# FoX heads first, differential heads last: reordering a mixer's attention stage

## The chip, the cores and the metric

The kernel runs on one core of a Trainium2 chip. A core has TensorE (PE, matrix products; its weight loads are listed as PEld), VectorE (DVE), ScalarE (ACT), GpSimd (POOL), SyncE (SP, which here only issues DMAs) and DMA queues. The metric is the device time of one execution in microseconds, the median of several runs; lower is better.

## The reference

Two layers, each of three residual blocks, then one RMSNorm, on x of 512 tokens by 1024 columns in float32:

```
x = x + 1/2 * SwiGLU_1(RMSNorm(x))
x = x + W_out [FoX_heads(h) ; Diff_heads(h)],   h = RMSNorm(x)
x = x + 1/2 * SwiGLU_2(RMSNorm(x))
```

The mixer, the middle block, has two groups of causal heads that read the same h through one input projection:

```
FoX, 8 heads of 64:  s = q k^T / 8 + cum[query] - cum[key];  o_f = softmax(s) v
                     cum = cumulative sum of log_sigmoid(h w_ff + bias)
Diff, 4 heads:       two maps of 64 on rope(q), rope(k);  v has 128 columns
                     o_d = (softmax(s1) - lam * softmax(s2)) v
                     o_d = RMSNorm(o_d) * subln * (1 - lambda_init)
out = [o_f ; o_d] W_out
```

So a FoX head needs the forget sums `cum`, a diff head needs rope, two softmaxes and, at its end, a norm over its 128 columns. Rows 0 to 511 of W_out belong to FoX, rows 512 to 1023 to diff.

## The kernel before

**Precision.** Every float32 product is made as three matmuls of a high and a low part (`mm3`, lines 399 to 403): high by high, high by low, low by high. Weights arrive in 128 x 1024 blocks of 512 KB and are split on ACT (high part, a cast, L83) and DVE (low part, a subtraction, L84). The feed-forward blocks use a seven-product scheme and are not touched by the change.

**Order of work.** The kernel is Python that emits instructions for each engine; a list scheduler of the compiler then fixes the order of each engine's queue, with the emitted order as priority and what is ready (in its own timing) ahead of what is not. A tile name has one buffer or a few; a new use waits until the old one is over. PSUM has 8 banks: 3 under the tag "a", 5 under "b".

**Weights.** `stream` lists all weight blocks in the order of use; `next_w(ahead)` hands out the next one and splits up to `ahead` further ones. In the mixer three buffers (G0 to G2) hold split blocks, three (R0 to R2) raw ones. The blocks of the input projection come from `w_in` in a fixed order, the first four of W_out go into the tiles XA0 to XA3, which until then hold h.

**The mixer.** `mixer` runs one projection (`proj`, `head`) and then a loop over 12 units, one per head, with 4 steps each (one for each block of 128 queries). A step s does, for unit s // 4, the scores and softmax of one query block (`softmax_step`); five steps later the transposes of the probabilities (`trans_step`); a step after that, a part of P·V (`pv_step`). Between these, `fill_to` draws on one long generator, `filler`, which holds all TensorE work that is not attention: projections, V of both kinds, gates, and the output projection as far as it can be had early. Filler is counted in matmuls: a projection is 48, V of one kind 96, the gates 16. `LEAD` is the filler issued ahead of the loop, `TARGET[u]` what must have been issued when unit u + 1 begins; what is left after the loop runs in `run(fill)`, then `out_rest` finishes the output projection and makes the next feed-forward's input forms.

**Before the change** units 0 to 3 are diff heads, 4 to 11 FoX heads. The filler is: projection d1, V of diff, d2, gates, d3 and f0 (with the gates' two later parts in between), V of FoX, f1 to f3, and 84 matmuls of output projection (`out_early`), 628 in all.

**Steps at the end of a head.** A FoX pair: ACT copies half of P·V, DVE adds, `split_o` splits the sum (L909 ACT, L910 DVE) into the operand `ovt[k]` of the output projection. A diff head: copy (L934), square (L936), split of the squares (L938, L939), then, a step later, `stats`: two matmuls with ones (L944, L945) and ACT (L946). After the last diff head `diff_norm` runs: the mean squares go to DRAM (L969) and back in another layout (L972), square root and reciprocal, to DRAM (L976), back as a broadcast to 128 partitions per head (L980), a multiplication (L982) and `split_o`. These are four DMA hops in a row.

**Evictions.** A projection's PSUM is scaled by DVE (FoX, L804), or put through rope (diff, L797, L798), where a DMA of four pieces turns the partitions (L801) and DVE adds (L802). Then q is split (L775, L776); k is first duplicated by DMA (L786), then split (L787, L788).

**Output projection.** `GROUPS` are the four 128 x 512 results of tokens 0 to 255, `GR2` those of tokens 256 to 511; each sums over k = 0 to 7, of which 0 to 3 are FoX and 4 to 7 diff. Before, early output takes k = 4, 5, 6, 7, 0, 1, 2 of the first half; `out_rest` adds k = 3, then makes the second half with k = 4 to 7, 3, 1, 0, 2.

Of the kernel before, what the change touches and what calls it, by code (L numbers as in the profile page):

```python
# [8 lines left out]
F32 = mybir.dt.float32  # L9
# [6 lines left out]
P = 128  # L16
# [13 lines left out]

LEAD = 70
TARGET = [128, 238, 290, 344, 393, 490, 497, 522, 525, 552, 560, 590, 604, 616]

# [19 lines left out]
def trunk(ctx, tc, xT, x, gains, gain_row, w_gu, w_dn, w_in, w_ff, w_out, fbias, lams, subln, consts, rope, out):  # L53
# [160 lines left out]
    len_x = list(range(KP)) * DEPTH  # L214
    OUT_K = (4, 5, 6, 7, 0, 1, 2)
    for n in range(2 * DEPTH):
        l = n // 2
        if n % 2 == 1:
            for i in range(24 + len(OUT_K)):
                k = OUT_K[i - 24] if i >= 24 else None  # L220
                tag = MIX[i % 3] if i < 24 else None if k >= 4 else MIX[(i - 28) % 3]
                stream.append(plain(w_in[l, i] if i < 24 else w_out[l, k], f"R{(i + 1) % 3}", tag))
        r = 0
        for kind, c in PARTS:
            if (n, kind, c) != (0, "u", 0):
                r = (gu_units if kind == "u" else dn_units)(n, c, part_order(kind, c), r)
# [368 lines left out]
    def mixer(l, n_next, mid):  # L595
# [27 lines left out]
        def y_pair(i):  # L623
            return ys[i // 4][:, i % 4], ys[i // 4][:, 4 + i % 4]
        os_ = [home(f"w{i}", [P, 2, S], F32, f"o{i}") for i in range(2)]

# [90 lines left out]
        def gates():  # L717
            pz = psum("a")
            for k in range(KT):
# [33 lines left out]
            yield 0  # L753
            pc = psum("a")
            for t in range(NB):
# [87 lines left out]

        cbs = {}

        def softmax_step(u, qb):
# [66 lines left out]
        def pv_step(u, kb):  # L913
# [97 lines left out]
        def out_early():  # L1011
            for i, k in enumerate(early):
                take_wo(k)
                for g in GROUPS[:3]:
                    if i == 0:
                        po1[g] = psum("a")
                    out_mm(po1[g], g, 0, k, i == 0, False)
                    yield 3
            g = GROUPS[3]
            po1[g] = psum("b")  # L1020
            for i, k in enumerate(early):
                out_mm(po1[g], g, 0, k, i == 0, False)
                yield 3
            take_wo(2)
            for g in GROUPS:
                out_mm(po1[g], g, 0, 2, False, False)
                yield 3

        def out_rest():
            busy.difference_update(LENT)  # L1030
            got = home("R2", [P, 1024], F32, "raw")
            sp.dma_start(out=got, in_=w_out[l, 3])
            w3 = home("G3", [P, 2, 1024], F32R, "wg")
            wo[3] = split(got, w3[:, 0], w3[:, 1])
            ensure(1)
            for g in GROUPS:
                out_mm(po1[g], g, 0, 3, False, True)
                out_add(po1[g], g, 0)
            GR2 = [(t, c) for c in range(2) for t in range(2)]
            po2 = {g: psum("a" if i < 3 else "b") for i, g in enumerate(GR2)}  # L1040
# [6 lines left out]
            for k in (3, 1):  # L1047
                for g in GR2:
                    out_mm(po2[g], g, 1, k, False, False)
            for g in GR2:  # L1050
                for k in (0, 2):
                    out_mm(po2[g], g, 1, k, False, k == 2)
                out_add(po2[g], g, 1)
            live.difference_update(MIX)
# [5 lines left out]

        early = [4, 5, 6, 7, 0, 1]

        def filler():
            yield from proj(("d", 1))
            yield from diff_v()
            yield from proj(("d", 2))
# [5 lines left out]
            for p_, n in ((proj(("d", 3)), 3), (proj(("f", 0)), 3)):  # L1072
# [4 lines left out]
            yield from fox_v()  # L1077
            for j in range(1, 4):
                yield from proj(("f", j))
# [366 lines left out]
```

## Time and profile before

| | us |
|---|---|
| median of 3 runs | 1865.27 (1864.65 to 1866.11) |
| the profiled execution | 1866.57 |
| its span, first to last instruction | 1864.8 |
| TensorE busy in the span | 1832.3 |
| DVE busy | 1611.7 |
| ACT busy | 1137.3 |

The first layer's mixer runs from about 346 to 600 us, its loop of heads from 374 to 569; the second layer's from about 1269 to 1524. Engine names are as above; "PE idle before" a line is time in which TensorE waited, with the instruction that released it. Matmuls overlap in the pipeline, so a single one is listed with some 0.39 us although one starts every 0.225 us, and a busy TensorE is not always one at its full rate. A window row gives busy time and, after x, the number of instructions that touch the window.

### The profile page before, as it was taken

What the parts mean: (1) busy time and instruction counts of PE and PEld (TensorE: products, weight loads), DVE (VectorE), ACT (ScalarE), POOL (GpSimd) and SP (SyncE); (2) the same over time, 40 slices, a digit from 0 to 9 for tenths busy, and PEclk for the clock granted to TensorE, in tenths of its full rate; (3) what the DMA queues carried; (4) which work ended last, traced back from release to release, by engine and by line L of the source; (5) the groups of instructions that cost most, each with busy time, mean ns of one, the idle gap of its engine ahead of it and who ended that gap; (6) DMA issues with size and microseconds to landing.
All of it is one profiled execution on the core that took longest, in us unless ns stands there. A gap on an engine that the chain in (4) does not pass through costs nothing.

```text
span 1864.8 us, 24528 instructions
## 1 busy us (share of the span) xinstructions
PE 1832.3 (98%) x8702; PEld 1495.9 (80%) x8702; DVE 1611.7 (86%) x2531; ACT 1137.3 (61%) x1819; POOL 128.1 (7%) x154
## 2 busy tenths in 40 slices
PE   9999999999999999999999999999999999999997
PEld 5888888778868889888878988887777688888886
DVE  7898899878686999898998989997877869898998
ACT  7555555557795755566575556545576957455564
POOL 2010000000000100100000000000000000000101
PEclk9999999999999999999999999999999999999999
DMA  9786655343336775777567667533433467756742
GB/s 314 207 225 192 186 141 145 99 127 103 108 97 180 204 203 152 193 213 193 136 179 205 170 163 213 157 115 112 120 97 109 128 170 193 214 142 186 222 115 89
DMA packets 95530, 303.80 MB, mean 163 GB/s; under 512 B 12568, under 2 KB 15128, under 8 KB 95408
## 3 DMA queue, kind: packets, MB, share of 16 engines
q1 hardware_dynamic: 74816, 232.15, 36.9%
q0 software_dynamic: 19296, 68.17, 20.6%
q10 hardware_dynamic: 1296, 1.93, 0.3%
q8 instruction: 68, 1.11, 0.2%
q14 instruction: 54, 0.44, 0.1%
HBM read 287.45 MB, written 2.16 MB: 155 GB/s over the span
## 4 chain that ended last, share of the span: by engine, by line
PE 82%; DVE 10%; ACT 6%; DMA 1%; issue 1%; SPq 0%; DVEq 0%; ACTq 0%
PE ps_c L401 12%; PE ps_c L402 12%; PE ps_c L403 12%; PE ps L401 8%; PE ps L402 8%; PE ps L403 8%; PE ps_a L401 3%; PE ps_a L402 3%; PE ps_a L403 3%; DVE wg L84 3%; PE ps_t L497 2%; DVE x L526 1%; PE ps_g L1265 1%; ACT wg L83 1%; ACT pg L876 1%
## 5 line engine op out<-in xcount | busy, mean ns | idle before, releaser
L83 ACT CAST wg<-raw 128x1024 fp32r<-128x1024 f32 (+1 forms) x525 | 537.8, 1032 | 480.0 <-PE ps L403 172.5
L84 DVE TENSOR_TENSOR wg<-raw,wg 128x1024 fp32r<-128x1024 f32 (+1 forms) x525 | 619.6, 1190 | 105.3 <-ACT wg L83 102.2
L401 PE MATMUL ps_c<-wg,xf 128*128 128x512 f32 (+1 forms) x736 | 277.9, 378 | 2.0 <-ACT wg L83 1.6
L402 PE MATMUL ps_c<-wg,xf 128*128 128x512 f32 (+1 forms) x736 | 277.1, 377 | 0.5 <-DVE wg L84 0.5
L403 PE MATMUL ps_c<-wg,xf 128*128 128x512 f32 (+1 forms) x736 | 276.4, 376 | 0.0
L401 PE MATMUL ps<-wg,xf 128*128 128x512 f32 (+1 forms) x552 | 210.1, 381 | 0.0
L402 PE MATMUL ps<-wg,xf 128*128 128x512 f32 (+1 forms) x552 | 207.3, 376 | 0.9 <-DVE wg L84 0.9
L403 PE MATMUL ps<-wg,xf 128*128 128x512 f32 (+1 forms) x552 | 206.7, 376 | 0.0
L401 PEld LDWEIGHTS ps_c<-wg,xf 128*128 128x128 f32 x736 | 138.7, 189 | 28.8 <-ACT wg L83 2.0
L402 PEld LDWEIGHTS ps_c<-wg,xf 128*128 128x128 f32 x736 | 139.0, 189 | 26.1 <-DVE wg L84 1.0
L403 PEld LDWEIGHTS ps_c<-wg,xf 128*128 128x128 f32 x736 | 138.9, 189 | 25.1
L134 POOL DMA_DIRECT2D raw<-w_gu x86 | 74.6, 867 | 1130.7 <-DMA raw<-w_gu 597.6
L401 PE MATMUL ps_c<-wg,hf 128*128 128x512 f32 x352 | 138.4, 393 | 4.0 <-DVE x L526 4.0
L402 PE MATMUL ps_c<-wg,hf 128*128 128x512 f32 x352 | 137.4, 390 | 0.0
L403 PE MATMUL ps_c<-wg,hf 128*128 128x512 f32 x352 | 137.1, 390 | 0.0
L526 DVE SCALAR_TENSOR_TENSOR x<-ps_c,x 128x512 f32<-128x512 f32 x192 | 124.0, 679 | 1.3 <-PE ps_c L403 1.2
L402 PEld LDWEIGHTS ps<-wg,xf 128*128 128x128 f32 x552 | 104.0, 188 | 18.9 <-DVE wg L84 1.3
L403 PEld LDWEIGHTS ps<-wg,xf 128*128 128x128 f32 x552 | 103.8, 188 | 18.9
L401 PEld LDWEIGHTS ps<-wg,xf 128*128 128x128 f32 x552 | 103.9, 188 | 18.0 <-ACT xf L83 0.4
L401 PE MATMUL ps_a<-XA,wg 128*128 128x512 f32 x256 | 106.0, 415 | 1.9 <-ACT XA L355 1.8
L401 PE MATMUL ps<-wg,hf 128*128 128x512 f32 x264 | 103.0, 390 | 0.0
L402 PE MATMUL ps<-wg,hf 128*128 128x512 f32 x264 | 103.0, 390 | 0.0
(290 smaller groups left out, 3549.6 us busy)
## 6 DMA issues: line engine op xcount, KB each, us to landing
raw<-w_gu SPq DMA_DIRECT2D x218, 512.0 KB, 4.6
raw<-w_dn SPq DMA_DIRECT2D x100, 512.0 KB, 4.2
raw<-w_gu POOLq DMA_DIRECT2D x86, 512.0 KB, 7.0
raw<-w_in SPq DMA_DIRECT2D x48, 512.0 KB, 3.3
raw<-w_dn POOLq DMA_DIRECT2D x40, 512.0 KB, 5.6
kdup<-qk_t SPq DMA_DIRECT2D x64, 128.0 KB, 2.4
raw<-w_out SPq DMA_DIRECT2D x16, 512.0 KB, 3.2
raw<-w_dn SPq DMA_DIRECT2D x20, 256.0 KB, 5.6
```

Of the source, the lines that this page charges most:

```text
L83: act.copy(out=hi, in_=src)
L84: dve.tensor_tensor(out=lo, in0=src, in1=rf(hi), op=ALU.subtract)
L134: pool.dma_start(out=t, in_=where(two, h)[1], accum_op=ALU.add)
L401: pe.matmul(p, lh, rh, start=start, stop=False, skip_group_check=again)
L402: pe.matmul(p, lh, rl, start=False, stop=False, skip_group_check=again)
L403: pe.matmul(p, ll, rh, start=False, stop=stop, skip_group_check=again)
L497: pe.transpose(pj[j][:, e * 256 + p * P:e * 256 + (p + 1) * P], hs[j][p][:, o:o + P], ident)
L526: dve.scalar_tensor_tensor(out=xc, in0=src, scalar=scale, in1=xc, op0=ALU.mult, op1=ALU.add)
L876: act.activation(out=e, in_=e, func=AF.Exp, scale=-1.0, bias=st[:, 0:1], accum_out=st[:, 2:3])
L1265: pe.matmul(pg[2 * half + j], gained(kp, e, half)[:, j * P:(j + 1) * P], w0[kp][:, e * S:(e + 1) * S], start=kp + e == 0, stop=kp == KP - ...
```

## The change

The units change places: FoX heads are units 0 to 7, diff heads 8 to 11. All that hangs on the order follows.

- The first projection is f0. The filler is: gates, V of FoX (with the gates' later parts inside), f1 to f3, d0, d1, V of diff, d2, d3, early output; 580 matmuls. `LEAD` is 92, `TARGET` new.
- Blocks of `w_in` and W_out are stored and streamed in that order; the k that go to XA0 to XA3 are 0 to 3.
- Early output is 36 matmuls, k = 0 to 3 for three groups; the splits of k = 4, 5, 6 follow. `out_rest` loads k = 7, then makes the fourth group with k = 0 to 3, the second half with k = 0, 1, the first half with k = 4 to 7, the second half with k = 2 to 7. All second-half sums and the fourth group lie in PSUM banks "b".
- The forget sums, which were broadcast into the rope tables' buffer, have their own (w1), and FoX outputs theirs (w0); the diff outputs take w0 and w1 over when those are done. V of diff lies in the other half of the y tiles. The gates use banks "b".

The number of matmuls, splits, evictions and bytes is the same.

```diff
-LEAD = 70
-TARGET = [128, 238, 290, 344, 393, 490, 497, 522, 525, 552, 560, 590, 604, 616]
+LEAD = 92
+TARGET = [137, 186, 213, 241, 267, 296, 321, 350, 410, 520, 560, 574, 580]
...
-    OUT_K = (4, 5, 6, 7, 0, 1, 2)
+    OUT_K = tuple(range(KT - 1))
...
-                tag = MIX[i % 3] if i < 24 else None if k >= 4 else MIX[(i - 28) % 3]
+                tag = MIX[i % 3] if i < 24 else None if k < 4 else MIX[(i - 28) % 3]
...
-        os_ = [home(f"w{i}", [P, 2, S], F32, f"o{i}") for i in range(2)]
+        os_ = {}
...
-                vh, vl = y_pair(t)
+                vh, vl = y_pair(4 + t)
...
-                wh, wl = next_w(2 if name != ("f", 3) else 1 - c)
+                wh, wl = next_w(2 if name != ("d", 3) else 1 - c)
...
-        units = [("d", h) for h in range(DIFF_H)] + [("f", h) for h in range(FOX_H)]
+        units = [("f", h) for h in range(FOX_H)] + [("d", h) for h in range(DIFF_H)]
...
+        cb_t = home("w1", [P, 2, S], F32, "cb")
+        fo_t = home("w0", [P, 2, S], F32, "fo")
...
-                    cbs[h] = rope_t[h % 2]
+                    cbs[h] = cb_t[:, h % 2]
...
+                if h % 2 == 0:
+                    os_[h // 2] = home(f"w{h // 2}", [P, 2, S], F32, f"o{h // 2}")
...
-                if h % 2 == 0:
-                    fo["u"] = pm_tile()
+                fo["u"] = fo_t[:, h // 2 % 2]
...
         def out_early():
-            for i, k in enumerate(early):
+            for k in range(4):
                 take_wo(k)
                 for g in GROUPS[:3]:
...
-            take_wo(2)
-            for g in GROUPS:
-                out_mm(po1[g], g, 0, 2, False, False)
-                yield 3
+            for k in (4, 5, 6):
+                take_wo(k)
...
+            g = GROUPS[3]
+            po1[g] = psum("b")
+            for k in range(4):
+                out_mm(po1[g], g, 0, k, k == 0, False)
+            GR2 = [(t, c) for c in range(2) for t in range(2)]
+            po2 = {}
+            for k in (0, 1):
+                for g in GR2:
+                    if k == 0:
+                        po2[g] = psum("b")
+                    out_mm(po2[g], g, 1, k, k == 0, False)
             for g in GROUPS:
-                out_mm(po1[g], g, 0, 3, False, True)
+                for k in (4, 5, 6, 7):
+                    out_mm(po1[g], g, 0, k, False, k == 7)
                 out_add(po1[g], g, 0)
...
-            for k in (4, 5, 6, 7):
+            for k in (2, 3):
                 for g in GR2:
-                    out_mm(po2[g], g, 1, k, k == 4, False)
+                    out_mm(po2[g], g, 1, k, False, False)
...
+            gt = gates()
...
+            fv = fox_v()
+            for n in (3, 18):
                 for _ in range(n):
-                    yield next(p_)
+                    yield next(fv)
                 next(gt)
-                yield from p_
...
+            yield from fv
+            for name in (("f", 1), ("f", 2), ("f", 3), ("d", 0), ("d", 1)):
+                yield from proj(name)
+            yield from diff_v()
+            for name in (("d", 2), ("d", 3)):
+                yield from proj(name)
             yield from out_early()
...
-        head = proj(("d", 0), first=True)
+        head = proj(("f", 0), first=True)
...
-        [qd[:, :4], v_blocks(dv), qd[:, 4:], qf[:, :2], v_blocks(fv), qf[:, 2:]], 1))
+        [qf[:, :2], v_blocks(fv), qf[:, 2:], qd[:, :4], v_blocks(dv), qd[:, 4:]], 1))
```

More of the change, by code (lines that the diff above doesn't have):

```diff
@@ L717, in gates @@
         def gates():
-            pz = psum("a")
+            pz = psum("b")
             for k in range(KT):
@@ L753, in gates @@
             yield 0
-            pc = psum("a")
+            pc = psum("b")
             for t in range(NB):
@@ L1011, in out_early @@
         def out_early():
-            for i, k in enumerate(early):
+            for k in range(4):
                 take_wo(k)
                 for g in GROUPS[:3]:
-                    if i == 0:
+                    if k == 0:
                         po1[g] = psum("a")
-                    out_mm(po1[g], g, 0, k, i == 0, False)
+                    out_mm(po1[g], g, 0, k, k == 0, False)
                     yield 3
[L1019 to L1022, printed above, removed]
-                yield 3
-            take_wo(2)
-            for g in GROUPS:
-                out_mm(po1[g], g, 0, 2, False, False)
-                yield 3
+            for k in (4, 5, 6):
+                take_wo(k)
         def out_rest():
@@ L1031, in out_rest @@
             got = home("R2", [P, 1024], F32, "raw")
-            sp.dma_start(out=got, in_=w_out[l, 3])
-            w3 = home("G3", [P, 2, 1024], F32R, "wg")
-            wo[3] = split(got, w3[:, 0], w3[:, 1])
+            sp.dma_start(out=got, in_=w_out[l, 7])
+            w7 = home("G3", [P, 2, 1024], F32R, "wg")
+            wo[7] = split(got, w7[:, 0], w7[:, 1])
             ensure(1)
+            g = GROUPS[3]
+            po1[g] = psum("b")
+            for k in range(4):
+                out_mm(po1[g], g, 0, k, k == 0, False)
+            GR2 = [(t, c) for c in range(2) for t in range(2)]
+            po2 = {}
+            for k in (0, 1):
+                for g in GR2:
+                    if k == 0:
+                        po2[g] = psum("b")
+                    out_mm(po2[g], g, 1, k, k == 0, False)
             for g in GROUPS:
-                out_mm(po1[g], g, 0, 3, False, True)
+                for k in (4, 5, 6, 7):
+                    out_mm(po1[g], g, 0, k, False, k == 7)
                 out_add(po1[g], g, 0)
-            GR2 = [(t, c) for c in range(2) for t in range(2)]
-            po2 = {g: psum("a" if i < 3 else "b") for i, g in enumerate(GR2)}
-            for k in (4, 5, 6, 7):
+            for k in (2, 3):
                 for g in GR2:
-                    out_mm(po2[g], g, 1, k, k == 4, False)
+                    out_mm(po2[g], g, 1, k, False, False)
             for kp in range(KP):
@@ L1046, in out_rest @@
             squares(0)
-            for k in (3, 1):
+            for k in (4, 5):
                 for g in GR2:
@@ L1050, in out_rest @@
             for g in GR2:
-                for k in (0, 2):
-                    out_mm(po2[g], g, 1, k, False, k == 2)
+                for k in (6, 7):
+                    out_mm(po2[g], g, 1, k, False, k == 7)
                 out_add(po2[g], g, 1)
@@ L1058, in run @@
                 pass
-        early = [4, 5, 6, 7, 0, 1]
         def filler():
-            yield from proj(("d", 1))
-            yield from diff_v()
-            yield from proj(("d", 2))
             gt = gates()
@@ L1071, in filler @@
                 yield w
-            for p_, n in ((proj(("d", 3)), 3), (proj(("f", 0)), 3)):
+            fv = fox_v()
+            for n in (3, 18):
                 for _ in range(n):
-                    yield next(p_)
+                    yield next(fv)
                 next(gt)
-                yield from p_
-            yield from fox_v()
-            for j in range(1, 4):
-                yield from proj(("f", j))
+            yield from fv
[4 more added lines that the diff above has]
+                yield from proj(name)
             yield from out_early()
-        head = proj(("d", 0), first=True)
+        head = proj(("f", 0), first=True)
         for _ in range(KT // 2):
```

## The prediction

> **What bounds the kernel now.** I read the page first (busy shares, chain), then busy time by stretch, TensorE's waits, and the groups of the attention stage.
>
> ```profile
> PE 1832.3 (98%) x8702; PEld 1495.9 (80%) x8702; DVE 1611.7 (86%) x2531; ACT 1137.3 (61%) x1819; POOL 128.1 (7%) x154
> PE 82%; DVE 10%; ACT 6%; DMA 1%; issue 1%; SPq 0%; DVEq 0%; ACTq 0%
> ```
>
> TensorE is busy 98% of 1864.8 us, and the change adds and removes no matmul. It can only move holes. The stretches show where the holes of one mixer are (columns: stretch, its length, then PE, PEld, DVE, ACT, POOL busy, granted clock, DMA share, GB/s):
>
> ```profile
> 629.00:645.00 16.00, 16.00 (x71) 13.03 (x70) 14.38 (x17) 8.13 (x9) 2.60 (x3) 1.00 0.91 252
> 374.00:505.80 131.80, 131.50 (x642) 105.28 (x641) 101.20 (x261) 89.58 (x190) 0.00 (x0) 1.00 0.37 111
> 505.80:569.40 63.60, 59.54 (x321) 45.26 (x320) 52.81 (x138) 54.52 (x132) 0.00 (x0) 1.00 0.41 131
> 530.00:540.00 10.00, 8.40 (x50) 6.32 (x49) 8.82 (x28) 9.79 (x27) 0.00 (x0) 1.00 0.49 138
> 570.00:580.00 10.00, 10.00 (x45) 8.28 (x45) 5.10 (x7) 4.12 (x7) 3.09 (x4) 1.00 0.96 288
> 1430.00:1481.00 51.00, 47.42 (x256) 36.09 (x254) 41.84 (x119) 44.58 (x112) 0.00 (x0) 0.97 0.32 96
> ```
>
> In a pure matmul stretch 71 matmuls take 16 us: 0.225 us for 512 columns, 0.44 ns a column. The attention loop runs from 374 to 569.4. Up to 505.8 (diff heads, then two FoX heads) TensorE is full. From 505.8, where the last six FoX heads run with hardly any filler, ACT is the bound: 9.79 of 10 us at 530. The ends of that stretch are these rows (scores' mask matmul of FoX unit 6, last P·V matmul):
>
> ```profile
> L841 PE MATMUL ps_b<-maskw,identb x24: 219/229/231, 506.0 to 555.9; 128*128 128x128 bf16 x24
> L928 PE MATMUL ps_b<-pt,vf x8: 278/323/387, 508.0 to 569.2; 128*128 128x256 f32 x8
> ```
>
> **Term A, what is removed.** A FoX unit needs on TensorE 2816 columns of scores, 2816 of P·V, 1280 of transposes and 512 of mask: 3.3 us. A diff unit needs 5632, 4224, 1280 and 1024 (sums of squares): 5.3 us. From unit 6 to the end the loop holds six units' scores (7.8 us with masks), seven of transposes and P·V (12.6) and 131 matmuls of filler (628 in all, 497 issued before unit 6; 29.5): 49.9 us in 63.6. The good stretch holds 427 of filler (96.1), four diff units (21.3), two FoX scores (2.6) and some 2 us of odds: 122 in 131.8, an overhead of 8%. At that rate the last six units would take 53.9. So **A = -9.7 us** a mixer if the hole closes.
>
> **Term B, the new tail.** With diff heads last, what ends the mixer is no longer the short FoX eviction. It is, in order: the eviction of the last projection (d3, done at filler 544 of 580, while its unit 11 is due at 560), unit 11's softmax, its P·V, then the diff norm with four DMA hops, which so far ran under FoX projections.
>
> The d eviction goes through two DMA rounds; one K half in the first layer:
>
> ```profile
> 408.62 0.69 DVE L797 TENSOR_TENSOR qk_b<-ps_a,rope 128x512 f32<-128x512 f32 x1 [0.42 <-PE ps_a L403]
> 409.34 2.41 SPq L801 DMA_DIRECT2D qk_c<-qk_b  x4
> 415.24 2.42 SPq L786 DMA_DIRECT2D kdup<-qk_t  x4
> 421.97 0.68 DVE L788 TENSOR_TENSOR qk<-kdup,qk 128x512 fp32r<-128x512 f32 x1
> ```
>
> That is 14.0 us from 408.62 to 422.65 in a crowded stage; without some 2 us behind other DVE work I take 12. The softmax of a diff unit is bound by ACT:
>
> ```profile
> L858 ACT ACTIVATE pg<-pg,st 128x128 f32<-128x128 f32 (+3 forms) x32 | 17.8, 557 | 15.0 <-DVE st L856 14.8
> L858 ACT ACTIVATION_READ_ACCUMULATOR pg<-pg,st 128x1 f32 x32 | 6.0, 189 | 0.0
> L863 ACT ACTIVATE pg<-pg,st 128x128 f32<-128x128 f32 (+3 forms) x16 | 9.0, 562 | 2.8 <-DVE st L862 2.6
> L897 ACT CAST pair<-ps_b 128x512 fp32r<-128x512 f32 (+2 forms) x36 | 16.9, 475 | 6.9 <-PE ps_b L888 6.5
> L936 ACT ACTIVATE osq<-ps_b 128x512 f32<-128x512 f32 x4 | 2.4, 596 | 0.0
> L938 ACT CAST pair<-osq 128x512 fp32r<-128x512 f32 x4 | 2.5, 627 | 0.0
> ```
>
> Per query block two exps and a scaling, 2 x 0.75 + 0.56 = 2.06; four blocks 8.2, and about 2.8 for the first block to pass scores, row minimum and combination: 11. Transposes, casts (0.475 each) and P·V of the last unit: 3.5. Copy, square, cast and subtract of its output: about 2.5. Then the norm, here from its first matmul to the split output of the first head, with the two last hops of the second layer:
>
> ```profile
> 495.98 0.40 PE L944 MATMUL ps_b<-pair,ones 128*32 128x512 f32 x1
> 496.64 0.68 ACT L946 ACTIVATE bb<-ps_b,eps_t 32x512 f32<-32x512 f32 x1 [0.17 <-PE ps_b L945]
> 511.55 1.41 DVE L982 SCALAR_TENSOR_TENSOR ou<-o,sub_s,rbd 128x512 f32<-128x512 f32 x2 [0.30 <-DMA rbd<-ms_d]
> 512.98 0.69 DVE L910 TENSOR_TENSOR y<-ou,y 128x512 fp32r<-128x512 f32 x1
> 1429.59 3.05 DMA ms_d<-nd
> 1432.66 3.31 DMA rbd<-ms_d
> ```
>
> 495.98 to 513.67 is 17.7 us. Sum: 12 + 11 + 3.5 + 2.5 + 17.7 = 46.7 us from d3's last matmul to the first output matmul of a diff head (k = 4).
>
> TensorE's work for that time: 36 matmuls of early output (8.1); 36 that the new order puts ahead of k = 4 (fourth group with k = 0..3, second half with k = 0, 1: 8.1); 24 of k = 2, 3, written behind k = 4 but ready earlier (5.4); three quarters of unit 10's scores and all of unit 11's (4.5); transposes, P·V and sums of units 10 and 11 (5.7), rest of unit 9 (0.7). 32.5, with 8% overhead 35.1. **B = +11.6.** The 24 count only if the compiler's list scheduler, which fixes each queue's order, draws them forward. It does such things: of the 16 transposes that the code writes ahead of the k = 3 products, eight run after them:
>
> ```profile
> 587.06 1.04 PE L339 MATMUL ps_t<-ident,x 128*128 128x128 f32 x8
> 587.86 0.47 PE L401 MATMUL ps_a<-wg,y 128*128 128x512 f32 x1
> 596.60 0.65 PE L339 MATMUL ps_t<-ident,x 128*128 128x128 f32 x4
> ```
>
> Bounds of B: 5 if d3 runs so far ahead of its unit that its 12 us hide under unit 10's softmax; 17 if the 24 stay behind.
>
> **Term C, the FoX units with filler.** Units 2 to 7 get some 28 matmuls each: TensorE 3.3 + 6.3 = 9.6, with overhead 10.4 us. DVE, from
>
> ```profile
> L874 DVE CUSTOM_DVE_ANT_0 pg<-ps_b,rope 128x128 f32<-128x128 f32 (+3 forms) x32 | 15.3, 484 | 3.1 <-PE ps_b L841 2.6 <-PE ps_a L403 0.3
> L898 DVE TENSOR_TENSOR pair<-ps_b,pair 128x512 fp32r<-128x512 f32 (+2 forms) x36 | 19.7, 551 | 8.4 <-ACT pair L897 8.2
> L84 DVE TENSOR_TENSOR wg<-raw,wg 128x1024 fp32r<-128x1024 f32 x21 | 25.7, 1222 | 4.0 <-ACT wg L83 3.9
> L797 DVE TENSOR_TENSOR qk_b<-ps_a,rope 128x512 f32<-128x512 f32 x6 | 4.0, 686 | 0.6 <-PE ps_a L403 0.6
> ```
>
> about 5.9 a unit plus, for a d projection of 48, 2 x 1.22 + 10 passes of 0.68 = 9.3, so 5.4 for 28: 11.3. Neighbouring instructions overlap (DVE's groups of the loop sum to some 174 us, busy is 154), so 10.0: 96% of TensorE's time in units 5 to 7, where FoX softmax meets rope evictions; ACT, the same way, 9.1. DVE will now and then be late: **C = +1** (0 to 4).
>
> **Moved at no cost.** The gates go ahead of the first unit, into the lead (92). Their DVE chain meets no softmax there, and 33 matmuls of V and 48 of projection f1 cover the forget sums' broadcast (4.2 us); without cover its 4.2 would be paid once. The rope DMAs and the gates' DMAs change places on SP's queue among loads that are three blocks ahead. The norm's hops now stand on SP ahead of the load of the last output weights and of the next feed-forward's: if all those wait for the norm, ten loads of 0.5 MB at 288 GB/s take 18 us, under 96 matmuls (21.6 us) that remain after it; POOL's accumulating loads follow these.
>
> ```profile
> raw<-w_gu SPq DMA_DIRECT2D x218, 512.0 KB, 4.6
> rope<-cum_d SPq DMA_DIRECT2D x16, 256.0 KB, 4.2
> ```
>
> **Term D, the clock.** In the second layer the starved stage was granted 0.97 over 51 us: 3 us at half clock, 1.5 us lost; the first layer lost none. A tail with holes in both layers: **D = +0.8** each. No wait of TensorE was long:
>
> ```profile
> PE ps_c L401 <- DVE x L526: 4.0, 4, 1.4
> PE ps_b L927 <- ACT pair L897: 3.9, 6, 0.9
> PE ps_c L401 <- ACT wg L83: 1.6, 1, 1.6
> ```
>
> The Trainium skill (TensorE: Matmul & The Clock Gate, "HAM oscillation — how this bites in real kernels") wants no idle gap beyond about 3.4 us, or the array drops to half clock; the trace shows the drop even with gaps of at most 1.6 us, so here the page is milder than the measurement. By its window, one unbroken gap in each norm would cost half of 3.4 us (an estimate from that page): D 1.7, the sum 1.8 us higher.
>
> **Sum.** -9.7 + 11.6 + 1 + 0.8 = +3.7 a mixer, +7.4 for two layers. The profiled execution took 1866.6 (span 1864.8 plus 1.8 around it), 1.3 above the median of the runs; 1865.3 + 7.4 = **1872.7**. Its own range: B from 9 to 15 gives 1867 to 1880.
>
> **Rivals.** (1) The tail is covered. TensorE takes filler ahead in the FoX units, d3's eviction hides under unit 10, B is 5, C and D nothing: -4.7 a mixer, **1856**. For it: in the loop as a whole TensorE has more to do (DVE was busy 101 of 132 us, ACT 90). Against: weights are split only two blocks ahead, and unit 9 with 110 of filler is too rich for ACT and DVE to stay busy. (2) The order stays as written: k = 4 stands in TensorE's queue before the 24, B is 17, the clock loses the second layer's 1.5 us in both: -9.7 + 17 + 1 + 1.5 = +9.8 a mixer, **1885**. It decides once the norm lands later than 36 matmuls (8.1 us) after its start, which 17.7 says; against it is the drawn-forward work above. (3) An even exchange, B = 8 to 9: **1865**. The order is then changed and the time is not.
>
> **Chances.** Forecast 0.42, rival (1) 0.34, (2) 0.13, (3) 0.11. A measurement of this kernel tells 0.2% (3.7 us) from no change. Of the forecast's 0.42, 0.06 lies inside 0.2%; with (3) 0.17 within, 0.34 faster, 0.49 slower. The range 1853 to 1886 takes in (1) and nearly all of (2).
>
> **What would show it.** A right: ACT below 9 of 10 us in all FoX units, TensorE full there. B right: 10 us or more of idle TensorE, or matmuls held by DMA rbd and DVE ou, between the last P·V and the first k = 4 product, and k = 2, 3 of the second half ahead of it. C: short waits of TensorE on DVE in units 5 to 7. D: granted clock under 1.00 at both mixers' ends. Wrong: a tail with under 6 us idle, or FoX units that TensorE waits through.

## The result, and the profile after

The changed kernel takes 1910.38 us (median of 4 runs, 1906.18 to 1913.87) against 1865.53 beside it: 1.0231 times the time before, 95% interval 1.0215 to 1.0248. The forecast, 1872.7, had the sign right and the size far off; its range ended at 1886.

First the page of the changed kernel: busy time, and the shares of the chain that ended last.

```profile
PE 1848.4 (97%) x8702; PEld 1509.8 (79%) x8702; DVE 1614.5 (84%) x2531; ACT 1135.5 (59%) x1815; POOL 128.7 (7%) x154
PE 86%; DVE 6%; ACT 4%; DMA 3%; issue 1%; SPq 0%; DVEq 0%; ACTq 0%; POOL 0%; POOLq 0%
```

TensorE is busy 16 us longer with the same 8702 matmuls, and the span is 1911.4, 46.6 more. Where does it lie? A mixer's length is read from the first matmul of its first projection to the first of the next feed-forward. In the timeline of the kernel before (start, duration, instruction):

```profile
346.37 0.51 PE L401 MATMUL ps_a<-XA,wg 128*128 128x512 f32 x1 [0.46 <-ACT XA L355]
599.83 0.39 PE L401 MATMUL ps_c<-wg,xf 128*128 128x512 f32 x1
1268.48 0.51 PE L401 MATMUL ps_a<-XA,wg 128*128 128x512 f32 x1 [0.68 <-ACT XA L355]
1524.99 0.39 PE L401 MATMUL ps_c<-wg,xf 128*128 128x512 f32 x1
```

and of the changed kernel:

```profile
347.62 0.50 PE L401 MATMUL ps_a<-XA,wg 128*128 128x512 f32 x1 [0.46 <-ACT XA L355]
628.41 0.39 PE L401 MATMUL ps_c<-wg,xf 128*128 128x512 f32 x1
1297.03 0.51 PE L401 MATMUL ps_a<-XA,wg 128*128 128x512 f32 x1 [0.67 <-ACT XA L355]
1571.88 0.39 PE L401 MATMUL ps_c<-wg,xf 128*128 128x512 f32 x1
```

The mixers grew from 253.5 to 280.8 and from 256.5 to 274.9 us: +27.3 and +18.3, together 45.7 of the 46.6. The stretches of the first one (columns as before: PE, PEld, DVE, ACT, POOL, granted clock, DMA share, GB/s):

```profile
374.00:536.00 162.00, 162.00 (x830) 132.16 (x828) 121.07 (x301) 113.45 (x253) 0.86 (x1) 1.00 0.43 129
536.00:552.00 16.00, 9.92 (x46) 7.59 (x44) 13.34 (x29) 11.44 (x24) 0.00 (x0) 0.92 0.57 172
552.00:576.00 24.00, 17.23 (x64) 12.78 (x64) 15.55 (x42) 17.06 (x40) 0.86 (x1) 0.70 0.27 94
576.00:592.00 16.00, 15.90 (x62) 12.46 (x62) 0.69 (x1) 2.20 (x4) 1.73 (x2) 0.89 0.66 131
592.00:602.00 10.00, 0.43 (x1) 0.43 (x2) 4.09 (x9) 1.02 (x2) 0.00 (x0) 0.60 0.24 82
```

All FoX units and the first diff units are now full: TensorE works 162.00 of 162 us. Everything is lost from 536 on. TensorE's longest waits (sum, times, longest) name what ended the idle time:

```profile
PE ps_a L401 <- ACT y L912: 14.8, 2, 9.6
PE ps_b L838 <- ACT qk L787: 8.0, 2, 5.1
PE ps_b L949 <- ACT pair L943: 6.6, 4, 1.9
```

(Lines behind the change have moved by 3 to 5: L838 still are scores; L912 is the split of a diff output, L949 the first sum of squares, L978 the reciprocal, L986 the scaling.) The first is the norm's end, the second the last projection's eviction. The timeline gives the tail's steps: d3's last matmul, the first score of unit 11, its last scaling, its last P·V product, the first sum of squares, the first k = 4 product.

```profile
531.77 0.39 PE L403 MATMUL ps_a<-XA,wg 128*128 128x512 f32 x1
552.56 0.58 PE L838 MATMUL ps_b<-qk 128*128 128x256 f32 x1 [5.06 <-ACT qk L787]
566.09 0.75 DVE L867 SCALAR_TENSOR_TENSOR pg<-pg,st 128x512 f32<-128x512 f32 x1
573.82 0.37 PE L927 MATMUL ps_b<-pt,y 128*128 128x256 f32 x1
576.06 0.42 PE L949 MATMUL ps_b<-pair,ones 128*32 128x512 f32 x1 [1.87 <-ACT pair L943]
601.57 0.80 PE L401 MATMUL ps_a<-wg,y 128*128 128x512 f32 x1 [9.61 <-ACT y L912]
```

| step of the tail, first layer, us | predicted | measured |
|---|---|---|
| d3's last matmul (ends about 532.0) to first score of unit 11 | 12 | 20.6 |
| softmax of unit 11 (to 566.84) | 11 | 14.3 |
| transposes and P·V (to 574.2) | 3.5 | 7.3 |
| copy, square, split (to 576.06) | 2.5 | 1.9 |
| norm, to the first k = 4 product | 17.7 | 25.5 |
| sum | 46.7 | 69.6 |

In the second layer the sum is 64.3. What stretched the norm stands in SP's, ACT's and DVE's timelines:

```profile
577.79 0.35 SPq L101 DMA_DIRECT2D raw<-w_gu  x1
578.50 0.24 SPq L973 DMA_DIRECT2D v_d<-bb  x1
585.88 0.48 SPq L976 DMA_DIRECT2D nd<-v_d  x1
587.83 0.23 ACT L977 ACTIVATE nd<-nd 64x32 f32<-64x32 f32 x1 [8.05 <-DMA nd<-v_d]
592.84 1.23 DVE L145 TENSOR_TENSOR raw<-raw 128x1024 f32<-128x1024 f32 x1 [16.11 <-DMA raw<-w_gu]
593.99 0.34 DVE L978 RECIPROCAL nd<-nd 64x32 f32<-64x32 f32 x1
595.21 0.48 SPq L980 DMA_DIRECT2D ms_d<-nd  x1
596.94 1.29 SPq L984 DMA_DIRECT2D rbd<-ms_d  x3
```

Two things. The last 2 KB of squares (v_d) are issued at 578.50, but the hop that needs them leaves at 585.88; in between, 512 KB blocks of the next feed-forward (w_gu), issued by SP and POOL from 569 to 578, are in flight. And the square root is done at 588.1, but the reciprocal starts at 593.99, behind an addition on a feed-forward block (L145) that stands ahead of it in DVE's queue and waits till 592.8 for POOL's load. Both belong to the next stage.

The eviction of d3 is late for other reasons. On DVE and SP:

```profile
539.14 1.40 DVE L776 SCALAR_TENSOR_TENSOR qk<-qk_t,qk 64x512 fp32r<-64x512 f32 x2 [0.28 <-ACT qk L775]
540.57 2.42 SPq L801 DMA_DIRECT2D qk_c<-qk_b  x4
546.17 2.67 SPq L786 DMA_DIRECT2D kdup<-qk_t  x4
```

Its K half passes rope on DVE at 535.28, 3.3 us after its last matmul, behind the softmax of unit 10. Its turning DMAs leave at 540.57, 0.03 us after DVE has split the Q half (L776). A feed-forward load stands ahead of them on SP, but it is not the cause: in run 1 below, which holds these loads back, they leave 5.3 us after the start of rope, as they do here. A temporary buffer that the split sets free is the likely link; no run tests it. The doubling leaves at 546.17, as soon as DVE's addition is done, which stood behind weight splits (L84); with two loads of output weights under way its last piece lands at about 552.3.

### The profile page after: what moved, and what is told of

Same layout as the page of the kernel before. It is cut to its first block, busy times and chain, and to the rows that moved or that the text cites. A ratio compares the mean times of both kernels' runs of the same rounds, so it can differ in the third digit from the quotient of the medians.

```text
span 1911.4 us, 24550 instructions
## 1 busy us (share of the span) xinstructions
PE 1848.4 (97%) x8702; PEld 1509.8 (79%) x8702; DVE 1614.5 (84%) x2531; ACT 1135.5 (59%) x1815; POOL 128.7 (7%) x154
## 4 chain that ended last, share of the span: by engine, by line
PE 86%; DVE 6%; ACT 4%; DMA 3%; issue 1%; SPq 0%; DVEq 0%; ACTq 0%; POOL 0%; POOLq 0%
PE ps_c L401 11%; PE ps_c L403 11%; PE ps_c L402 11%; PE ps L403 8%; PE ps L402 8%; PE ps L401 8%; PE ps_a L401 4%; PE ps_a L402 3%; PE ps_a L403 3%; PE ps_t L497 2%; DVE wg L84 2%; DVE x L526 1%; DMA raw<-w_gu 1%; PE ps_g L1271 1%; PE ps_b L891 1%
## 5 line engine op out<-in xcount | busy, mean ns | idle before, releaser
L84 DVE TENSOR_TENSOR wg<-raw,wg 128x1024 fp32r<-128x1024 f32 (+1 forms) x525 | 621.3, 1195 | 114.7 <-ACT wg L83 111.6
L401 PEld LDWEIGHTS ps<-wg,xf 128*128 128x128 f32 x552 | 104.0, 188 | 17.7
L401 PE MATMUL ps_a<-XA,wg 128*128 128x512 f32 x256 | 110.2, 431 | 1.8 <-ACT XA L355 1.8
```

What stands on the lines that cost most here:

```text
L84: dve.tensor_tensor(out=lo, in0=src, in1=rf(hi), op=ALU.subtract)
L401: pe.matmul(p, lh, rh, start=start, stop=False, skip_group_check=again)
```

## The experiments

Four theories: (1) the next stage's loads and weight additions collide with the tail; (2) d3's eviction comes too late for unit 11; (3) idle time puts TensorE to half clock, which stretches the rest; (4) the norm's chain is simply too long to stand at the end. All ratios are to the kernel before on the same chip. It took 1867.4 to 1867.8 us there, 1.8 to 2.3 more than beside the changed kernel, whose own four runs spread over 7.7 us. The gains below are plain differences from 1910.4; against the kernel before beside each run they are some 2 us larger. In the diffs, `issue_after(x)` puts an instruction behind x in the queue of x's engine.

**1. Loads behind the norm.** `hold` is true from the mixer's start until its last part.

```diff
+            if hold[0] and not must:
+                return None
...
-            ensure(1)
+            hold[0] = False
+            with tc.issue_after(nrm.pop("rbd").ins):
+                ensure(1)
```

> Edit: nothing of the computation is left out. The loads of the next feed-forward's weight blocks that the mixer asks for ahead of need are held back, and those that the end of the mixer asks for are issued on SP only behind the third broadcast of the diff norm. Theory 1 (the prefetch collides with the tail): the norm, from its first sum-of-squares product to the first k = 4 product, falls from 25.5 and 21.0 us (first and second layer) to about 18, the landing of the squares' rows in DRAM from 7.0 to about 2.4 us, no feed-forward weight subtraction (raw<-raw) stands on DVE between square root and reciprocal, and the d3 eviction falls from 17.3 to about 14; in all some -18 us against the changed kernel, about 1892. If the loads are then late for the feed-forward, TensorE shows new waits on wg or raw after 602 of up to 10 us a mixer. Rival, the chain itself is too long (theory 4): the norm's steps keep their length when alone and the gain is under 3 us. Rival, the clock (theory 3): with the same idle gaps broken up the same, the half-clock stretches stay and the gain is only that of the shorter gap.

Measured: 1893.7 us, ratio 1.0139 (1.0122 to 1.0156): 16.7 less than the changed kernel. The same steps of the norm in its timelines:

```profile
574.93 0.42 PE L953 MATMUL ps_b<-pair,ones 128*32 128x512 f32 x1 [1.82 <-ACT pair L947]
572.08 5.77 SPq L977 DMA_DIRECT2D v_d<-bb  x2
578.81 0.48 SPq L980 DMA_DIRECT2D nd<-v_d  x1
580.90 0.34 DVE L982 RECIPROCAL nd<-nd 64x32 f32<-64x32 f32 x1 [5.30 <-ACT nd L981]
590.68 0.39 PE L404 MATMUL ps_a<-wg,y 128*128 128x512 f32 x1
```

The norm takes 15.8 us instead of 25.5: the hop to DRAM 1.0 (577.85 to 578.81) instead of 7.1, nd's hop to reciprocal 2.1 instead of 8.1. From the last P·V product to k = 4 it is 17.9 and 17.8 us in the two layers (27.8 and 23.3 in the changed kernel). No new wait for feed-forward weights appears. The expected gain for the eviction did not come: the last P·V product stands 225.7 us after the mixer's start in the first layer (226.2) and 227.4 in the second (226.0). Theory 1 holds, for the norm alone.

**2. The addition on DVE alone.** Loads unchanged; only L145 goes behind the norm's refinement.

```diff
-                dve.tensor_tensor(out=src, in0=get("5", h), in1=src, op=ALU.add)
+                with tc.issue_after(gate.pop()) if gate else nullcontext():
+                    dve.tensor_tensor(out=src, in0=get("5", h), in1=src, op=ALU.add)
```

> Edit: only one instruction of each mixer is moved: the DVE addition on a feed-forward block (raw<-raw) that stood ahead of the norm's reciprocal is put behind the last DVE instruction of the square root's refinement. The loads stay where they are. Nothing is left out. If the order of DVE's queue was a cause by itself, the reciprocal starts some 0.6 us after the square root instead of 5.6 us (first layer) and 2 us (second), about -7 us in all with a little clock: 1903. What then remains of the 16.7 us, some 9 to 10, belongs to the loads' share of the DMA engines and SP's queue. If the loads alone were the cause, the next hops (to DRAM and back) are slowed instead and the gain is under 2 us.

Measured: 1903.0, ratio 1.0189 (1.0172 to 1.0206), -7.4.

```profile
583.70 0.48 SPq L979 DMA_DIRECT2D nd<-v_d  x1
585.98 0.35 DVE L981 RECIPROCAL nd<-nd 64x32 f32<-64x32 f32 x1 [9.30 <-ACT nd L980]
587.22 0.48 SPq L983 DMA_DIRECT2D ms_d<-nd  x1
591.80 4.59 SPq L987 DMA_DIRECT2D rbd<-ms_d  x4
```

The reciprocal follows its hop by 2.3 us, but the hops stay slow: 4.6 us from ms_d to rbd, 1.7 in the run above (582.14 to 583.85) and in the changed kernel, where the loads had landed by then. Of theory 1's 16.7 us, one in-order instruction makes 7.4; the other 9.3, by subtraction, belong to the loads beside the hops. The norm's length agrees: 20.8 and 20.5 us in the two layers here, 15.8 and 15.7 in run 1, 9.8 apart.

**3. The last projection a unit earlier.**

```diff
-TARGET = [137, 186, 213, 241, 267, 296, 321, 350, 410, 520, 560, 574, 580]
+TARGET = [140, 190, 226, 262, 298, 334, 370, 410, 470, 544, 560, 574, 580]
```

> Edit: nothing is left out; the targets of the filler are raised (140, 190, 226, 262, 298, 334, 370, 410, 470, 544 in place of 137, 186, 213, 241, 267, 296, 321, 350, 410, 520 for the first ten units), so that the last projection is done at the start of unit 10, a unit earlier than in the changed kernel. Theory 2 (the last eviction comes too late): TensorE's wait of 9.6 and 5.1 us ahead of unit 11's scores (first matmul after qk) goes to under 3 us in both layers, and with its half clock some 8 us a mixer are gone: about 1894. Rival (the filler is only moved): the softmax of units 10 and 11, bound by ACT, then has no filler beside it, TensorE waits there on pg or pair instead, and the time is within 4 us of the changed kernel's. The norm's part (25.5 and 21.0 us) is not touched by any theory.

Measured: 1900.1, ratio 1.0177 (1.0162 to 1.0192), -10.3. TensorE's waits:

```profile
PE ps_a L401 <- ACT y L912: 10.8, 2, 7.9
PE ps_b L949 <- ACT pair L943: 10.2, 6, 2.4
PE ps_b L838 <- ACT qk L787: 0.4, 2, 0.2
```

The wait for qk went from 8.0 to 0.4 us, as theory 2 says, but the gain is 10, not 16: the wait ahead of the sums of squares rose from 6.6 to 10.2. The last two units now have 36 matmuls of filler beside them by the targets, where they had 60.

**4. Without the norm's round trip.**

```diff
-            sp.dma_start(out=v, in_=v_d.rearrange("h (a b) -> (h a) b", b=32))
-            act.activation(out=y, in_=v, func=AF.Sqrt)
...
-                dve.scalar_tensor_tensor(out=u, in0=ov[h], scalar=sub_s, in1=rbd, op0=ALU.mult, op1=ALU.mult)
+                dve.scalar_tensor_tensor(out=u, in0=ov[h], scalar=sub_s, in1=ov[h], op0=ALU.mult, op1=ALU.bypass)
```

> Edit: the diff norm's way through DRAM and its scaling of the outputs are left out (the outputs are multiplied by the per-channel weight alone; the sums of squares are still made by TensorE). It is a measurement of what the norm at the end costs, by any cause. Theory 4 and theory 1 alike: TensorE's wait of some 10 us ahead of the k = 4 products goes, with the half clock after it, in both layers: -25 us, about 1885; what is left above the kernel before (some 20 us) belongs to d3's eviction and unit 11's softmax. If theory 2 or 3 had nothing to do with the rest, the time would fall to 1865. If the norm were hidden by the 60 drawn-forward matmuls, the time would stay within 4 us.

Measured: 1885.5, ratio 1.0096 (1.0081 to 1.0111), -25, as expected. So the norm, by any cause, makes 25 of the 45 us, and the eviction and the last softmaxes the other 20 (net of what the FoX units gained).

**5. Matmuls of zeros in the tail.**

```diff
+            for i in range(20):
+                for g in GROUPS[:3]:
+                    pe.matmul(po1[g], pt3[0][:, 0:P], wo[3][0][:, 0:S], start=False, stop=False)
```

> Edit: nothing is left out; in each mixer 60 matmuls with an all-zero weight tile (13.5 us at full rate) are added to three of the output sums after the early output products. They add zero and only keep TensorE at work. Theory 3 (the half clock costs some 8 us a mixer): where these fill idle time in the last units, the granted clock of the tails rises from 0.6-0.7 to near 1.00 and the time falls by up to 8 us a mixer. Rival (half clock costs nothing there because the chain of ACT, DVE and DMAs sets the end): the clock rises and the time stays. Rival (they run where TensorE had work): +13.5 us a mixer, 1937, if none fall into idle time.

Measured: 1903.0, ratio 1.0191 (1.0176 to 1.0206): 7.4 less, with 120 matmuls more. The stretch that was granted 0.70 and held 64 matmuls:

```profile
552.00:576.00 24.00, 23.71 (x122) 18.60 (x122) 14.89 (x42) 18.51 (x41) 1.73 (x2) 1.00 0.45 126
```

In the first layer the last P·V product comes 4.4 us earlier (221.8 us after the mixer's start, not 226.2), in the second no earlier (226.1, not 226.0). Not all of the 4.4 can be the clock's: 1.0 lies ahead of d3's last matmul, and the last softmax takes 12.3 us in place of 14.3, but 12.8 in run 4, which has no zeros. What stands out is the work behind the last scaling, up to the last P·V product: 5.6 us in both layers, where the changed kernel and runs 1, 3 and 4 take 6.9 to 7.3. The clock granted there rose from 0.55 and 0.58 to 1.00. In the second layer the first score of unit 11 comes 1.9 us later, which takes this back. From the last P·V product to k = 4 it is 3.6 and 2.4 us shorter; that stretch is mostly a chain of DMAs, and the edit also moved the loads, so this part can't be put down to the clock. Theory 3 is borne out at 1.4 us a layer, not at the 8 expected.

**6. Loads and targets together.**

> Edit: the two edits of the earlier runs together: the feed-forward loads behind the norm's broadcast, and the filler's targets raised. Nothing is left out. The loads alone gave -16.7 us against the changed kernel, the targets alone -10.3. If the two causes are separate places of one chain (the norm; the last eviction) they add up: 1910.4 - 27 = 1883. Rival: they share a part, because the raised targets move the eviction out of the way of the same loads, or because the tail is bound by ACT's softmax once the eviction is early: 1888 or more. Rival: with both gone the tail is covered: 1870 or less.

Measured: 1882.4, ratio 1.0081 (1.0066 to 1.0096), 28 less, the sum of the two, as for separate places of one chain. Two stretches of its first mixer:

```profile
535.00:570.00 35.00, 25.97 (x115) 18.04 (x115) 27.87 (x81) 29.72 (x72) 0.86 (x1) 0.90 0.35 91
570.00:585.40 15.40, 15.40 (x62) 12.41 (x61) 5.18 (x12) 4.48 (x7) 0.00 (x0) 0.89 0.35 102
```

TensorE is busy through the whole norm (570 to 585.4), with the 60 products that need no diff output. The idle time is now in units 10 and 11, where ACT is busy 29.7 of 35 us.

**7. The same with 30 matmuls of zeros.**

> Edit: the two edits together, and 30 matmuls with an all-zero weight tile a mixer (6.8 us at full rate) after the early output; they add zero, nothing is left out. Theory 3 (what is left is in part half clock): the granted clock of the tails comes nearer 1.00 and the time is 2 to 6 us below that of the two edits without them. Rival (no idle time left for them): they cost up to 13.5 us. Rival (they fill idle time and the clock has no price): within 2 us.

Measured: 1881.3, ratio 1.0075 (1.0060 to 1.0090), 1.1 less than without them: no difference.

```profile
535.00:570.00 35.00, 30.91 (x152) 22.82 (x151) 28.50 (x82) 30.06 (x74) 0.86 (x1) 1.00 0.35 93
```

The granted clock went from 0.90 to 1.00. The last P·V product does come 1.5 and 1.4 us earlier after the mixer's start, but from there to the next feed-forward the two layers take 0.8 and 1.7 us more, and TensorE's waits for y, the split diff outputs, rise from 1.6 to 5.0 us. What the clock gains ahead of the norm is lost behind it.

**8. The two edits without the round trip.** The norm's lines are left out as in 4.

> Edit: the two edits together, and the diff norm's way through DRAM and its scaling left out (the outputs are multiplied by the per-channel weight alone). It measures what the norm still costs when nothing collides with it. If the 60 drawn-forward matmuls now cover it (that trace shows TensorE full from the last P.V on, but for 1.6 us), the time is within 4 us of the 1882.4 of the two edits, and the rest above the kernel before (15 us) belongs to the softmax of units 10 and 11 without filler. Rival: the norm still costs: 1875 or less.

Measured: 1874.2, ratio 1.0037 (1.0022 to 1.0052). The expectation, no change, fails: 8.2 less. What vanished from the waits is mostly one line, 10.2 us in run 3 and in run 6:

```profile
PE ps_b L953 <- ACT pair L947: 1.9, 2, 0.9
```

The traces differ mostly behind the last P·V product: from it to the next feed-forward run 6 takes 41.7 and 42.1 us, this run 37.7 in both layers. Up to it each mixer is 1.3 us shorter.

**9. Sums of squares later in TensorE's queue**, to see if that line is the price.

```diff
+                if h < DIFF_H - 1:
+                    later.append(lambda: None)
                 later.append(stats)
...
+                    with tc.issue_after(nrm["g3"].ins) if "g3" in nrm else nullcontext():
+                        pe.matmul(pq[0:32], ones[:, 0:32], sh_, start=True, stop=False)
```

> Edit: the two edits together, and the sums of squares of the diff outputs later in TensorE's queue: those of units 8 to 10 one step later, those of unit 11 behind nine products of the early output. Nothing is left out. Without the norm's round trip the two edits gained 8.2 us more, though their trace shows no wait for the norm's broadcast but 1.6 us; what vanished there was TensorE's wait of 10.2 us in all for pair (ACT's split of the squares) ahead of the sums. If this in-order wait is the rest of the norm's price, it goes and the time falls by 4 to 8 us, to about 1876. Rival: the waits move to the transposes and P.V behind, and the norm's start, 1 us later, is paid at its end: within 2 us of 1882.

Measured: 1893.0, ratio 1.0131 (1.0114 to 1.0148): 10.5 slower, worse than the rival allowed. The line is gone from the waits, but others stand there:

```profile
PE ps_b L895 <- DVE pg L871: 9.1, 6, 2.7
PE ps_a L404 <- ACT y L916: 7.2, 4, 2.9
```

Transposes now wait for scalings, and k = 4 products, though first ready at 584.0, wait in between for later heads. So the run does not show the wait for pair to be a price of its own; the chain now waits elsewhere. What in the norm makes the 8.2 us of run 8 stays open.

**10. Output weights split later**, behind the last sums of squares.

```diff
-            for k in (4, 5, 6):
-                take_wo(k)
...
+            with tc.issue_after(nrm["a_end"].ins), tc.issue_after(nrm["d_end"].ins):
+                for k in (4, 5, 6):
+                    take_wo(k)
```

> Edit: the two edits together, and the splits of the output weights k = 4 to 7 (1.05 us on ACT and 1.22 us on DVE each) are moved out of units 10 and 11 to behind the last unit's sums of squares, into the time in which ACT and DVE wait for the norm's hops. Nothing is left out. If units 10 and 11 are bound by ACT and DVE, the last P.V comes some 3 to 4 us earlier in each mixer and the time falls to about 1875. Rival: those units are bound by the chain from score to P.V of single blocks, in whose gaps the splits lie: within 2 us of 1882. Rival: the splits delay square root or reciprocal: slower.

Measured: 1884.2, ratio 1.0091 (1.0076 to 1.0106), within 2 us of run 6, yet not as the rival has it. The last P·V product does come earlier, 216.2 us after the mixer's start in the first layer instead of 219.9. But the norm gets longer, 17.7 and 18.7 us to the first k = 4 product instead of 15.8 and 14.1, and outlasts the 60 products that cover it: waits of 8.4 us in all for y take the gain back. One reason stands on SP: the load of the last output weights, which waits for a buffer that the first moved split frees, now stands ahead of nd's hop, which leaves 2.7 us after v_d is issued, not 1.0.

**11 and 12. Two FoX heads last.** FoX heads 0 to 5, the diff heads, FoX heads 6 and 7, with run 1's loads.

```diff
-        units = [("f", h) for h in range(FOX_H)] + [("d", h) for h in range(DIFF_H)]
+        units = [("f", h) for h in range(6)] + [("d", h) for h in range(DIFF_H)] + [("f", 6), ("f", 7)]
```

> Edit: an order between the two kernels: FoX heads 0 to 5, the four diff heads, FoX heads 6 and 7 last, with projections in that order, k = 3 of the output projection held back till after the loop, new targets, and the feed-forward loads behind the norm's broadcast. Nothing is left out. The diff norm then runs beside the last two FoX units, and filler still lies beside six FoX units. If the price of the new order was the norm and the late eviction at the end, the tail is short again: the mixer keeps most of the 9 us that the filled FoX units gained and ends 1850 to 1860, faster than both. Rival: the last two FoX units have no filler, are bound by ACT and DVE as before, and the norm's hops and the last FoX eviction meet there: 1865 to 1880.

Measured: 1901.1, ratio 1.0181 (1.0166 to 1.0196). TensorE's two longest waits, and ACT's timeline at their end:

```profile
PE ps_b L404 <- DVE pg L969: 12.2, 2, 10.1
PE ps_b L404 <- ACT fot L968: 10.5, 1, 10.5
```

```profile
578.71 0.62 ACT L916 CAST y<-ou 128x512 fp32r<-128x512 f32 x1 [11.71 <-DVE ou L995]
579.36 0.58 ACT L968 COPY fot<-ps_b 64x512 f32<-64x512 f32 x1
```

The last FoX heads' copy (fot) stood on ACT behind a diff output that waited 11.7 us for the norm: the same fault, between two chains of the mixer itself. Run 12 puts the scaling of the diff outputs behind the last FoX split, and all feed-forward loads behind the broadcast:

```diff
+        with tc.issue_after(nrm["s", 3].ins):
+            for h in range(DIFF_H):
+                nrm["ones"](h)
```

> Edit: the order with two FoX heads last as before, but the four diff outputs are scaled on DVE only behind the split of the last FoX pair, and every feed-forward load stands on SP behind the third broadcast. Nothing is left out. In the run without this, TensorE waited 10.1 and 10.5 us for the last FoX pair's copy and sum (fot, pg), which stood on ACT and DVE behind diff outputs that waited for the broadcast (landed 6.4 us after its issue). If that order of two queues and those loads were its price, both waits go and the time falls by about 20 us, to 1880. Rival: TensorE is then held by the norm itself or by softmax in the last units without filler, and less than 8 us come back (1893).

Measured: 1884.2, ratio 1.0086 (1.0069 to 1.0103), 16.9 less. Both waits went; new ones stand in their place, such as this:

```profile
PE ps_t L345 <- DVE x L1023: 7.4, 2, 3.8
```

No version ran faster than the kernel before.

## Why the prediction was wrong, and where it was right

**Term A holds.** The hole of the last FoX units is closed: TensorE is full from 374 to 536, and DVE and ACT are busy 75% and 70% of it. By columns at 0.44 ns its products come to some 151.5 us of the 162.0 (an estimate from the timeline), 7% over, near the 8% assumed; the last FoX stretch before had 48.8 in 63.6, 30% over. The sum has one slip: at 3328 columns a unit, six units' scores with masks are 8.8 us, not 7.8, which makes A some -8.7. No run isolates it, but a tail that cost more than the whole difference is in line with it: 69.6 us of tail less the predicted 35.1 of work is 34.5, less the predicted 9.7 is 24.8, and the mixer grew by 27.3.

**Term C was zero, not 1.** No wait on DVE appears in the FoX units; TensorE is busy 162.00 of 162 us there.

**Term B failed, and in it the latency.** Two parts of its description were right: the eviction, the last softmax and the norm are what TensorE waits for, and the 24 products k = 2, 3 were drawn forward (the stretch from 576 to 592 above: 62 matmuls, busy 15.90 of 16 us, 57 of them early products in one run), so that rival (2)'s reason, an order kept as written, is wrong though its time was nearer. But 46.7 us became 69.6. The durations came from a trace in which these steps ran under projections, away from the feed-forward's loads, and they were added as if nothing new would stand beside them. 17.7 for the norm is even too much for an undisturbed one (15.8 in run 1); 12 for the eviction, which took 20.6, left out what stands ahead of it on DVE: the softmax of unit 10, the Q half's split and weight splits. In the other company of run 3 it is 14.7. The 3.5 for unit 11's transposes and P·V became 7.3, partly at half clock: run 5 takes 1.4 us of that away.

**"Moved at no cost" is the step that failed most.** It asked what happens if the feed-forward's loads wait for the norm, and found cover for that. The other direction was not asked: nothing makes those loads wait. They have no input from the mixer, so they were issued into the norm's hops, and with them came an addition in DVE's queue. Undoing this alone gives 16.7 us back; undoing the late eviction, which is term B's, 10.3; both 28. Together that is the distance from the changed kernel to 1882, which lies inside the range given, 1853 to 1886.

**The rest.** At 1882.4 the kernel is 15 us above the one before, 7.5 a mixer, where the forecast had 3.7. Run 8 puts 8.2 of the 15 on the norm, which is what remains of theory 4. The rest, by subtraction, is the softmax of units 10 and 11 with little filler less the gain in the FoX units; the prediction had seen this hole in the eviction of d3, and closing that moved it there.

**Term D** was 0.8 a mixer. Run 5 bears out 1.4 in each layer of the changed kernel and leaves room for 2.0 and 0.5 more in the last softmax; once the collisions are gone, run 7 shows no gain in the end. In the first layer the granted clock was 0.50 from 552.5 to 556, behind the wait of 5.1 us, and 0.50 from 601.5 to 606, behind the one of 9.6. The Trainium skill (TensorE: Matmul & The Clock Gate, "HAM oscillation — how this bites in real kernels") ties the drop to gaps beyond some 3.4 us; the gaps of 5.1 and 9.6 us here agree with that. But the clock was back at 1.00 from 560 to 564 and fell to 0.50 again from 566.84 to 570, where no wait of TensorE was longer than 1.4 us, so the drop also came behind short waits, as it did in the kernel before (0.50 from 1465 to 1468).

**Rivals.** (1), a covered tail, needed the eviction under unit 10 and a short norm; run 6 made both true, and the time was still 1882, not 1856: the idle time had moved to the softmax of the last units, and the norm still cost some of it (run 8). (3), an even exchange, has nothing for it: no version came within 0.2% of the kernel before.

## What to carry to other kernels

When a latency-bound chain is moved to the end of a stage, look at what of the next stage is free to start there: its prefetches share the DMA engines with the chain's small hops, and its first arithmetic can land ahead of the chain in an in-order queue. Price a moved chain with what will be its neighbours, not with the durations of its old place. And an order of issue that a scheduler chooses by its own timing needs an explicit edge wherever a long load might be late.

## What the runs showed of the hardware that was not expected

A 2 KB write to DRAM needed 7.1 us until the next hop could leave while 512 KB loads were under way, against 1.0 without them. The Trainium skill (DMA: Bandwidth & Descriptors, "Issuing engines are not separate DMA queues") says that DMAs from SP and POOL end up on the same 16 engines and interleave; the trace agrees, with loads from both under way.

Matmuls of an all-zero operand kept the granted clock at 1.00 where it had been 0.70 or 0.90, so they count as work for the clock. The raised clock shortened the last transposes and P·V by 1.2 to 1.4 us in each mixer, and in run 7 the time as a whole stayed the same, because TensorE then waited longer for the norm (5.0 us for y in place of 1.6).
